# Hybrid encoder layer: when the mLSTM's normalised outputs are transposed, and how many norms are under way

## The chip, the cores and the metric

The kernel runs on one core of a Trainium2 chip. The metric is the device time of one execution in microseconds (us). A time that stands for a kernel is the median of several runs; a profile shows one further execution, which has its own time.

## The reference, cut to what matters

The layer takes two sequences, a prompt of 1024 tokens and a sample of 2048, each with 16 learned meta tokens in front. One projection of the normalised input feeds two branches: attention over a neighbourhood of a grid, and an mLSTM that runs forwards and backwards in 4 heads of 128. Both branches are gated and projected, merged by sigmoid gates, projected once more, normalised and added to the input. This is the part of the mLSTM around the change:

```python
h = (h_f + h_b)[:, :, P:].transpose(0, 2, 1, 3)
h = jax.nn.sigmoid(o_pre.astype(f32)).reshape(B, L, ML_HEADS, ML_HEAD_DIM) * h
mu = jnp.mean(h, axis=-1, keepdims=True)
var = jnp.mean(jnp.square(h - mu), axis=-1, keepdims=True)
h = (h - mu) * lax.rsqrt(var + EPS)
return (h.reshape(B, L, ML_WIDTH) * head_g.astype(f32)).astype(v.dtype)
...
yb = (_mlstm_branch(ml_qk, ml_v, ml_g, ml_o, ml_conv_w, ml_head_g) * jax.nn.silu(ml_z)) @ w_b
```

## The kernel before, in words

**Two streams of work.** The program is written by two Python generators. `dense` writes the large products: the input projection by groups of columns (L422 to L424 token-major, L153 to L155 through `mm3` feature-major), and the final blocks of 512 tokens (`final`, L1255 on: a merge of the two branches, whose products are evacuated from PSUM by VectorE at L1291, L1293 and L1295, and then the output products at L1312 to L1314). `sparse` writes the mLSTM of a sequence (`ml`) and the attention (`na`), in the order of STEPS: mLSTM of the prompt, attention of the prompt, mLSTM of the sample, attention of the sample. Each `yield` of `sparse` ends a *piece* and names a cost (for the mLSTM's outputs A_A = 1.87); `run` then takes as many pieces from `dense` as this cost pays for (six products of 128x512 are 1.41). So a piece of the mLSTM is always followed by products of `dense`, and TensorE runs in the order in which the pieces were written.

**Who orders what.** `manual_schedule` holds for TensorE alone: its queue is the order of the program. The queues of VectorE (DVE), ScalarE (ACT), GpSimd (POOL) and of the DMA issues (SP, SPq in the profile) are ordered by a planner that simulates the program when it is built. On the chip each queue is run in the order that the planner left.

**The mLSTM of one sequence.** For each of four heads, `ml_states` (L915 on, three pieces a block of 256 tokens) makes the states of all chunks, backwards in order, and `ml_outputs` (L1009 on) makes the outputs, a block b of 256 tokens (two chunks) at a time, in six pieces. In iteration b the pieces are: (1) the scores of block b on TensorE (`scores`, PSUM tag sc, one bank) and the start of the next convolution, (2) the products of block b-1's first chunk with state and values (`back`, PSUM tags tr and sm) and the low parts of the scores (L1109), (3) loads, (4) the second chunk (`back`) and the split of the next q (L1049 to L1053), (5) the split of the next k, a decay, and `finish` of block b-1, (6) the other decay and the split of block b's state and values (`state`, L1079 and L1090). The prompt has 4 blocks a head, the sample 8; there is one iteration more than blocks.

`finish` divides the sums into the tile hb (L1144 on ACT, L1145 on DVE). One hb takes two blocks, so every second iteration ends a tile of 512 tokens by one head and puts a generator `ml_norm` (L1192) on the list `norms`. There are 24 such norms: numbers 0 to 7 for the prompt (two a head) and 8 to 23 for the sample (four a head). hb has two buffers. The tiles of the two gates, tog and szg, share two buffers.

**What a norm does, by its own steps.** First step: the sigmoid gate (L1196), four bn_stats (L1200) and four bn_aggr (L1202) on DVE. Second: variance plus epsilon (L1204) and `rsqrt8`, eleven small DVE instructions each of which needs the one before (L139 to L144, three rounds of L142 to L144). Third: four scalings (L1208) and the product with the other gate (L1209), on DVE; then eight empty steps. Last: four transposes on TensorE (L1214, PSUM tag tr, two buffers), the copy back into hb with the head's gain (L1215 on ACT) and the store to HBM (L1216, issued by SP).

**When the steps come.** `ml` drives them (L888 to L903). At each piece the current norm makes one step. A norm that has been put on the list is taken off at the first piece whose step finds no norm under way, and makes its first step one piece after that. It is put on the list in piece 5 of an even iteration b, so its first step comes in piece 6, and its eleventh, with the transposes, in piece 4 of iteration b+2, right behind that piece's `back`. The next norm is put on the list one piece later, so at most one is under way. A norm that is open at the end of a head makes its steps in the pieces of the next head's `ml_states`. After the last head the rest of the steps get a piece each (L902).

Of the kernel before, what the change touches and what calls it, by code (L numbers as in the profile page):

```python
# [120 lines left out]
class K:  # L121
# [748 lines left out]
    def ml(self, s):  # L870
        tc, nc = self.tc, self.nc
        T = SEQLEN[s]
        NB = T // BL
        with tc.tile_pool(name=f"mg{s}", bufs=1, side="right", reuse_waits="tile") as keep:
            with tc.tile_pool(name=f"mt{s}", bufs=1, side="right", reuse_waits="tile") as mp:
                self.tri = keep.tile([P, 2, P], F32, name="tri")
                nc.sync.dma_start(self.tri, self.i["tri"])
                self.trim = keep.tile([P, 2, CB, P], F32, name="trim")
                for j in range(CB):
                    nc.sync.dma_start(self.trim[:, :, j, :], self.i["trimask"])  # L880
                g = []
                yield from self.ml_gates(s, keep, mp, g)
            with tc.tile_pool(name=f"ml{s}", bufs=1, side="right", reuse_waits="tile") as mp:
                self.vas = [mp.tile([P, CB, 130], F32, name=f"va{j}") for j in range(3)]
                for va in self.vas:
                    nc.gpsimd.memset(va[:, :, 128:129], 1.0)
                    nc.gpsimd.memset(va[:, :, 129:130], 0.0)
                norm = iter(())  # L888
                for h in range(4):
                    sts = {}  # L890
                    for cost in self.ml_states(mp, s, h, g, NB, sts):
                        next(norm, None)
                        yield cost
                    norms = deque()
                    for cost in self.ml_outputs(mp, s, h, g, NB, sts, norms):
                        if next(norm, "end") == "end" and norms:
                            norm = norms.popleft()
                        yield cost
                    if norms:
                        for _ in norm:  # L900
                            pass
                        norm = norms.popleft()  # L902
                for _ in norm:  # L903
                    yield A_A
        self.done.add(("ml", s))

# [285 lines left out]
    def ml_norm(self, mp, s, h, q, hb, tz):  # L1192

        nc = self.nc
        to, sz = tz
        nc.vector.scalar_tensor_tensor(hb, to, 1.0, hb, op0=ALU.add, op1=ALU.mult)  # L1196
        bs = mp.tile([P, 4, 6], F32, name="bs", bufs=1)
        mv = mp.tile([P, 4, 2], F32, name="mv", bufs=1)
        for j in range(4):
            nc.vector.bn_stats(bs[:, j], hb[:, j])  # L1200
        for j in range(4):
            nc.vector.bn_aggr(mv[:, j], bs[:, j])  # L1202
        yield
        nc.vector.tensor_scalar(mv[:, :, 1], mv[:, :, 1], 4.0 * EPS, None, op0=ALU.add)  # L1204
        rs = self.rsqrt8(mp, mv[:, :, 1], [P, 4])
        yield
        for j in range(4):
            nc.vector.tensor_scalar(hb[:, j], hb[:, j], mv[:, j, 0:1], rs[:, j:j + 1], op0=ALU.subtract, op1=ALU.mult)  # L1208
        nc.vector.tensor_tensor(hb, hb, sz, op=ALU.mult)  # L1209
        for _ in range(8):  # L1210
            yield
        pt = self.psum("tr", [P, 4, P])
        for j in range(4):
            nc.tensor.transpose(pt[:, j, :], hb[:, j], self.ident)  # L1214
        nc.scalar.activation(hb, pt, AF.Copy, scale=self.hg[:, h:h + 1])  # L1215
        nc.sync.dma_start(self.YB[s][h][:, 512 * q:512 * q + 512], hb.rearrange("p a b -> p (a b)"))  # L1216
# [295 lines left out]
```

## Time and profile before

| | |
|---|---|
| median of 3 runs | 2899.09 us (2895.03 to 2908.92) |
| profiled execution, its time | 2904.42 us |
| profiled execution, its span | 2902.7 us |
| mean granted TensorE clock | 0.989 |
| TensorE products (PE) busy | 2817.5 us, 97% of the span, 17488 instructions |
| TensorE weight loads (PEld) busy | 2510.5 us, 86% |
| DVE busy | 1745.0 us, 60%, 4816 instructions |
| ACT busy | 1297.8 us, 45% |

The span runs from the first to the last instruction; the execution's own time is 1.7 us longer. A line of a group names the line of the kernel, the engine, the operation, the tile written and the tiles read, how often it came, its busy time and mean time, and how long its engine sat idle before it and for whom. In a timeline the first column is the start in us from the span's start and the second the duration. In the table by stretches each engine has its busy time and number of instructions, and PEclk is the share of the full clock that TensorE was granted.

### The profile page before, as it was taken

The numbers are of one execution on the slowest core, as the hardware profiler recorded it, in microseconds if no ns is written. First come the engines' busy times: TensorE is split into PE (matmuls) and PEld (weight loads), VectorE is DVE, ScalarE is ACT, GpSimd is POOL, SyncE is SP. The second block draws the span as 40 slices with busy tenths as digits, with TensorE's granted clock in tenths as the row PEclk, the third lists the DMA queues.
The fourth block names the chain that finished last, engine by engine and source line by source line (L and its number), as shares of the span: only waits on it lengthen the run. The fifth ranks groups of instructions, "written<-read, shape, count | busy, mean of one in ns | idle before, by whom it ended". The sixth has DMA issues, their size and how long they took to land.

```text
span 2902.7 us, 49301 instructions
## 1 busy us (share of the span) xinstructions
PE 2817.5 (97%) x17488; PEld 2510.5 (86%) x17488; DVE 1745.0 (60%) x4816; ACT 1297.8 (45%) x3114; POOL 16.2 (1%) x104
## 2 busy tenths in 40 slices
PE   7999999999999999999998999999999999999998
PEld 6998898899789988888887998898888888879888
DVE  4232575666556754467669877563555557777843
ACT  4112555444443444355555545443444445545421
POOL 0000000000000000000000000000000000000000
PEclk9999999999999999999999999999999999999999
DMA  9655666754775553577678899546669659888875
GB/s 360 213 178 180 209 226 229 270 185 160 246 235 172 185 171 125 174 251 273 233 247 324 284 326 310 160 156 193 188 196 288 202 160 271 256 287 257 292 256 196
DMA packets 387736, 661.88 MB, mean 228 GB/s; under 512 B 50624, under 2 KB 199440, under 8 KB 387488
## 3 DMA queue, kind: packets, MB, share of 16 engines
q1 hardware_dynamic: 386368, 656.03, 68.5%
q0 software_dynamic: 1120, 2.69, 0.4%
q8 instruction: 138, 2.26, 0.3%
q14 instruction: 110, 0.90, 0.1%
HBM read 447.97 MB, written 210.61 MB: 227 GB/s over the span
## 4 chain that ended last, share of the span: by engine, by line
PE 84%; DMA 8%; DVE 5%; issue 1%; ACT 1%; SPq 1%; DVEq 0%; ACTq 0%
PE pj L153 14%; PE pj L154 14%; PE pj L155 14%; PE pj L422 6%; PE pj L424 6%; PE pj L423 6%; PE sm L712 3%; PE pj L1312 3%; PE tr L700 3%; PE pj L1314 3%; PE pj L1313 3%; DMA tg<-gt 1%; PE sc L675 1%; PE sc L676 1%; DMA um<-ud 1%
## 5 line engine op out<-in xcount | busy, mean ns | idle before, releaser
L153 PE MATMUL pj<-xh,whi 128*128 128x512 f32 (+1 forms) x1824 | 717.6, 393 | 0.6 <-ACT xh L324 0.6
L154 PE MATMUL pj<-xl,whi 128*128 128x512 f32 (+1 forms) x1824 | 700.7, 384 | 1.3 <-DVE xl L325 1.3
L155 PE MATMUL pj<-xh,wlo 128*128 128x512 f32 (+1 forms) x1824 | 699.2, 383 | 0.0
L422 PE MATMUL pj<-whi,xh 128*128 128x256 f32 (+3 forms) x1576 | 451.2, 286 | 0.0
L423 PE MATMUL pj<-wlo,xh 128*128 128x256 f32 (+3 forms) x1576 | 445.0, 282 | 0.0
L424 PE MATMUL pj<-whi,xl 128*128 128x256 f32 (+3 forms) x1576 | 444.9, 282 | 0.0
L155 PEld LDWEIGHTS pj<-xh,wlo 128*128 128x128 f32 x1824 | 344.2, 189 | 72.2
L153 PEld LDWEIGHTS pj<-xh,whi 128*128 128x128 f32 x1824 | 344.5, 189 | 57.7 <-ACT xh L324 0.7
L154 PEld LDWEIGHTS pj<-xl,whi 128*128 128x128 f32 x1824 | 345.0, 189 | 56.6 <-DVE xl L325 1.6
L422 PEld LDWEIGHTS pj<-whi,xh 128*128 128x128 f32 (+1 forms) x1576 | 295.2, 187 | 1.4
L423 PEld LDWEIGHTS pj<-wlo,xh 128*128 128x128 f32 (+1 forms) x1576 | 294.6, 187 | 1.1
L424 PEld LDWEIGHTS pj<-whi,xl 128*128 128x128 f32 (+1 forms) x1576 | 294.4, 187 | 0.9
L683 ACT ACTIVATE prb<-sc,mx 128x384 f32<-128x384 f32 (+2 forms) x192 | 120.4, 627 | 228.8 <-DVE mx L679 219.4
L1312 PE MATMUL pj<-whi,mh 128*128 128x256 f32 x768 | 220.0, 286 | 0.0
L1314 PE MATMUL pj<-whi,mlo 128*128 128x256 f32 x768 | 217.2, 283 | 0.9 <-DVE mlo L1295 0.9
L1313 PE MATMUL pj<-wlo,mh 128*128 128x256 f32 x768 | 216.7, 282 | 0.0
L703 DVE TENSOR_TENSOR pts<-tr,pts 96x512 fp32r<-96x512 f32 (+2 forms) x192 | 131.9, 687 | 119.7 <-ACT pts L702 118.1
L431 DVE TENSOR_TENSOR stT<-pj,bb 128x256 f32<-128x256 f32 (+3 forms) x197 | 83.5, 424 | 139.4 <-PE pj L424 136.8
L702 ACT ACTIVATE pts<-tr 96x512 fp32r<-96x512 f32 (+2 forms) x192 | 114.3, 595 | 117.1 <-PE tr L700 116.6
L679 DVE CUSTOM_DVE_ANT_1 sc<-sc,gt 128x384 f32<-128x384 f32 (+2 forms) x192 | 118.7, 618 | 76.0 <-PE sc L676 68.4
L153 PE MATMUL pj<-yh,whi 128*128 128x512 f32 x384 | 157.4, 410 | 4.7 <-DVE tg L1291 4.6
L718 DVE TENSOR_TENSOR yg<-sm,yg 64x128 f32<-64x128 f32 x384 | 108.2, 282 | 77.5 <-ACT yg L716 70.0
(232 smaller groups left out, 5119.5 us busy)
## 6 DMA issues: line engine op xcount, KB each, us to landing
whi<-wh SPq DMA_DIRECT2D x176, 512.0 KB
wlo<-wl SPq DMA_DIRECT2D x176, 512.0 KB
wraw<-wu SPq DMA_DIRECT2D x64, 512.0 KB
wh<-whi SPq DMA_DIRECT2D x64, 512.0 KB
wl<-wlo SPq DMA_DIRECT2D x64, 512.0 KB
gt<-st SPq DMA_DIRECT2D x96, 256.0 KB
tg<-gt SPq DMA_DIRECT2D x96, 256.0 KB
xh<-xh SPq DMA_DIRECT2D x6, 2048.0 KB
```

The lines of the kernel that those rows point to most:

```text
L153: mm(out, ah, bh, start=start, stop=False)
L154: mm(out, ah, bl, start=False, stop=False)
L155: mm(out, al, bh, start=False, stop=stop)
L422: nc.tensor.matmul(o, xh, wh, start=k == 0, stop=False)
L423: nc.tensor.matmul(o, xh, wl, start=False, stop=False)
L424: nc.tensor.matmul(o, xl, wh, start=False, stop=k == KT - 1)
L679: nc.vector.tensor_tensor_reduce(out=so, in0=so, in1=gt[:, g0:g0 + ns, c0:c0 + 32], op0=ALU.add, op1=ALU.min, scale=-1.0, scalar=3.0e38, a ...
L683: nc.scalar.activation(pr_[:, :N].rearrange("p (b a c) -> p b a c", b=4, c=8), sc[:, :N].rearrange("p (a b c) -> p b a c", b=4, c=8), AF.E ...
L703: nc.vector.tensor_tensor(pts[:ks, :, 1, :], pt[:ks], pts[:ks, :, 0, :].bitcast(F32), op=ALU.subtract)
L1312: nc.tensor.matmul(o, mh[:, k, xs], wh, start=k == 0, stop=False)
L1313: nc.tensor.matmul(o, mh[:, k, xs], wl, start=False, stop=False)
L1314: nc.tensor.matmul(o, ml[:, k, xs], wh, start=False, stop=k == KT - 1)
```

## The change

Two things are changed.

In `ml` the one current norm becomes a list of norms under way. At each piece every norm on the list makes one step, and one that ends leaves the list. Nothing waits for an earlier norm to end: a norm put on the list in piece 5 makes its first step in that same piece. The drain at the end of a head (for a norm still open when another is waiting) goes away. After the last head every round makes two steps of each open norm for one piece of cost A_A.

In `ml_norm` the empty steps between the third step and the transposes become twelve instead of eight. A norm now has fifteen steps; the last comes in piece 1 of iteration b+3, right behind that piece's `scores`, or in the next head's `ml_states`. The transposes of a norm come there while the next norm, put on the list in piece 5 of iteration b+2, is already under way.

```diff
-                norm = iter(())
+                norms = deque()
+
+                def step():
+                    for x in tuple(norms):
+                        if next(x, "end") == "end":
+                            norms.remove(x)
+
                 for h in range(4):
                     sts = {}
                     for cost in self.ml_states(mp, s, h, g, NB, sts):
-                        next(norm, None)
+                        step()
                         yield cost
-                    norms = deque()
                     for cost in self.ml_outputs(mp, s, h, g, NB, sts, norms):
-                        if next(norm, "end") == "end" and norms:
-                            norm = norms.popleft()
+                        step()
                         yield cost
-                    if norms:
-                        for _ in norm:
-                            pass
-                        norm = norms.popleft()
-                for _ in norm:
+                while norms:
+                    step()
+                    step()
                     yield A_A
...
         nc.vector.tensor_tensor(hb, hb, sz, op=ALU.mult)
-        for _ in range(8):
+        for _ in range(12):
             yield
         pt = self.psum("tr", [P, 4, P])
```

## The prediction, made before the changed kernel was built or run

> **What bounds the kernel now.** The page first: busy time of the engines.
>
> ```profile
> PE 2817.5 (97%) x17488; PEld 2510.5 (86%) x17488; DVE 1745.0 (60%) x4816; ACT 1297.8 (45%) x3114; POOL 16.2 (1%) x104
> ```
>
> TensorE has a product in flight for 2817.5 us of a span of 2902.7 us. The change neither adds nor takes away a product, so it can only act on the 85 us in which PE has none, and on the clock behind such gaps. The view of PE's waits names them:
>
> ```profile
> PE pj L322 <- DVE xr L311: 18.9, 2, 12.6
> PE tr L1214 <- DVE hb L1209: 12.5, 1, 12.5
> PE tr L700 <- DVE prb L692: 11.3, 3, 6.1
> ```
>
> The first is the start of the program, which the change doesn't touch. The second is the norm's transposes: 24 norms, and one single wait of 12.5 us, for the product L1209 just ahead of them. The third lies in the attention. So 23 of the 24 norms have their transposes at a time when hb is ready, and for them later transposes gain nothing.
>
> The place of the wait, in PE's timeline and in the table by stretches (PE, PEld, DVE, ACT and POOL busy, then PEclk, DMA share, GB/s):
>
> ```profile
> 1554.44 0.28 PE L155 MATMUL sm<-vh,sl 128*128 128x130 f32 x1
> 1567.26 1.08 PE L1214 MATMUL tr<-ident,hb 128*128 128x128 f32 x4 [12.54 <-DVE hb L1209]
> ```
>
> ```profile
> 1500.00:1554.70 54.70, 54.56 (x286) 46.13 (x285) 51.19 (x145) 36.05 (x89) 0.20 (x2) 1.00 0.97 349
> 1554.70:1567.30 12.60, 0.06 (x2) 0.07 (x2) 12.60 (x42) 6.92 (x18) 0.00 (x0) 0.68 0.84 303
> 1567.30:1573.00 5.70, 5.70 (x16) 4.62 (x17) 5.18 (x26) 1.96 (x5) 0.00 (x0) 0.50 0.58 182
> 1573.00:1580.00 7.00, 7.00 (x39) 5.95 (x37) 6.96 (x17) 3.34 (x7) 0.00 (x0) 1.00 0.60 213
> 1580.00:1680.00 100.00, 97.37 (x661) 89.22 (x660) 83.52 (x232) 54.50 (x156) 0.30 (x2) 1.00 0.87 302
> ```
>
> The reader is to see two things. While PE waits, DVE is busy for 12.60 of 12.60 us: the transposes wait for a loaded engine, not for a chain that stands still. And behind the wait PE runs 5.70 us at PEclk 0.50, so that 2.85 us more are lost. The place costs 12.5 + 2.85 = 15.4 us in all, 0.53% of the time. That is the most that the change can win by what it says.
>
> **What the change moves, and the sum.** All is reckoned for norm 13, the one that waits.
>
> *Transposes later: 6.2 us.* They come in piece 1 of an iteration, behind the scores, instead of piece 4 of the one before, behind `back`. What lies between on PE is 24 products of 128x512 and six of the scores. One iteration earlier, at full clock, the same stretch is
>
> ```profile
> 1540.72 0.45 PE L153 MATMUL pj<-yh,whi 128*128 128x512 f32 x1
> ...
> 1546.35 0.22 PE L153 MATMUL sc<-qh,kh 128*128 128x128 f32 x1
> ...
> 1546.96 0.45 PE L153 MATMUL pj<-yh,whi 128*128 128x512 f32 x1
> ```
>
> 1546.96 - 1540.72 = 6.24 us. If L1209 ended when it ends now, the wait would be 12.5 - 6.2 = 6.3 us.
>
> *But DVE gets work in those 6.2 us.* The order of its queue round the wait (each line's first figure is the start):
>
> ```profile
> 1550.13 0.19 DVE L139 TENSOR_SCALAR nwy<-mv 128x4 int32<-128x4 int32 x1
> ...
> 1551.48 0.77 DVE L1102 TENSOR_TENSOR um<-um,sc 128x256 f32<-128x256 f32 x2
> ...
> 1552.53 0.71 DVE L1293 TENSOR_TENSOR tg<-tg 128x512 f32<-128x512 f32 x1
> 1553.14 0.19 DVE L140 TENSOR_SCALAR nwy<-nwy 128x4 int32<-128x4 int32 x1
> ...
> 1554.88 0.18 DVE L142 SCALAR_TENSOR_TENSOR nwt<-nwy 128x4 f32<-128x4 f32 x1
> 1554.95 0.71 DVE L1295 TENSOR_TENSOR mlo<-tg,mh 128x512 fp32r<-128x512 f32 x1
> ...
> 1556.07 0.71 DVE L1291 SCALAR_TENSOR_TENSOR tg<-tg,pj 128x512 f32<-128x512 f32 x1
> 1556.67 0.19 DVE L143 TENSOR_TENSOR nwt<-nwt,mv 128x4 f32<-128x4 f32 x1
> ...
> 1566.41 0.70 DVE L1209 TENSOR_TENSOR hb<-hb,szg 128x512 f32<-128x512 f32 x1
> ...
> 1570.94 0.69 DVE L1291 SCALAR_TENSOR_TENSOR tg<-tg,pj 128x512 f32<-128x512 f32 x1
> ...
> 1575.46 0.69 DVE L1291 SCALAR_TENSOR_TENSOR tg<-tg,pj 128x512 f32<-128x512 f32 x1
> ```
>
> The eleven small steps of the reciprocal root take 0.2 us each but stand 1.7 to 3.0 us apart, because evacuations, splits and scores stand between them. Today the evacuations of the 24 products behind the wait come after L1209 (1570.94, 1575.46), because PE stood still. In the new order PE makes these products first, and the planner may let their evacuations in ahead of L1209: two L1291, one L1293, one L1295 (0.71 each) and the two L1102 of the scores (0.77), 3.6 us. The ends are 0 (all stay behind) and 3.6 (all go ahead). The nearest row is L1291 at 1556.07, which went between two steps of the root 2.3 us after its products ended; so I take 3.6 and keep 0.
>
> *The norm's steps one piece earlier.* The first step is written in piece 5 instead of 6. What it needs is the second half of hb:
>
> ```profile
> 1538.40 0.35 DVE L1145 SCALAR_TENSOR_TENSOR hb<-num,den,hb 128x128 f32<-128x128 f32 x1
> ...
> 1540.87 0.69 DVE L1196 SCALAR_TENSOR_TENSOR hb<-tog,hb 128x512 f32<-128x512 f32 x1
> ```
>
> hb is there at 1538.75 and L1196 starts at 1540.87. So the chain can start between 0 and 2.1 us earlier; other ready work will stand ahead of it here too, and I take half, 1.0.
>
> *The sum.* New wait: 12.5 - 6.2 + 3.6 - 1.0 = 8.9 us, a gain of 3.6. The ends are 12.5 - 6.2 - 2.1 = 4.2 (gain 8.3) and 12.5 - 6.2 + 3.6 = 9.9 (gain 2.6). The half clock stays: a much shorter stop has one behind it as well.
>
> ```profile
> 1233.00:1235.00 2.00, 0.09 (x1) 0.00 (x0) 2.00 (x7) 2.00 (x8) 0.10 (x1) 1.00 0.47 114
> 1235.00:1242.00 7.00, 5.82 (x26) 5.52 (x27) 5.48 (x18) 4.45 (x16) 0.00 (x0) 0.51 0.45 113
> ```
>
> Two microseconds with almost no product, and then 7 us at 0.51, worth 3.5 us. [...]
>
> *What costs nothing, and what hides it.* The number of instructions is the same. PSUM's tr pair: the transposes now stand between two `back`s six pieces apart, with more room than now. The gates' buffers are read by the first and third step as before. The last norm of each sequence: two steps a piece make its transposes come after six pieces instead of nine, so the lead of hb shrinks. It is now
>
> ```profile
> 754.90 0.69 DVE L1209 TENSOR_TENSOR hb<-hb,szg 128x512 f32<-128x512 f32 x1
> ```
>
> ```profile
> 770.89 0.60 PE L1214 MATMUL tr<-ident,hb 128*128 128x128 f32 x4
> ```
>
> 15.3 us over nine pieces, so a third less leaves some 10: no wait. The store L1216 and hb's buffer: the store goes out 6.2 us later, and the ACT write of the norm after next waits for its landing. The tightest pair, and a transfer of the same 256 KB on the chain of waits:
>
> ```profile
> 1776.78 0.35 SPq L1216 DMA_DIRECT2D yb<-hb  x1
> ```
>
> ```profile
> 1784.94 0.69 ACT L1144 ACTIVATE hb<-num,den 128x128 f32<-128x128 f32 x2
> ```
>
> ```profile
> 1537.93 6.49 DMA tg<-gt
> ```
>
> 1776.8 + 6.2 + 6.5 = 1789.5, so ACT could stand 4.6 us at that one norm, with everything in its queue behind it (the next block's decay, the sums of `back`). ACT is 45% busy and PE asks for these only pieces later; I take 0 and keep 4.6 for the range. On SP, the store is moved past about two loads of the next block, each 0.3 to 0.4 us to issue: nothing.
>
> On the profiled execution this gives 2904.4 - 3.6 = 2900.8 us. Its own time lies 5.3 us above the median of 2899.1 (runs from 2895.0 to 2908.9), and the prediction is for the median: **2895.5 us**, 2890 to 2898 by the ends.
>
> **The rivals.** *The wait goes altogether.* The product would have to end at 1554.7 + 6.2 = 1560.9 instead of 1567.1. For it: the planner makes DVE's order anew, and between 1554.7 and 1567.3 DVE also did work of the next head, which nothing waits for. Against it: DVE was full. Gain 15.4 us, 2883.7 us; it decides if the planner's order brings the chain 6.2 us forward.
>
> *The wait is handed on.* DVE is busy 51.19 + 12.60 + 5.18 + 6.96 + 83.52 = 159.5 us between 1500 and 1680; without the 15.4 us that is 97% of what is left. If DVE is the limit there, PE stops for the same work a little later, at `tg` or `mlo`: 2899 us, and the change doesn't do what it says.
>
> *Slower: the norm pushes the state split back.* The first step now stands ahead of `state(b)` in the program instead of behind it, and the second beside it. PE needs the split (vl, L1079) two pieces later in `back`, and its lead is thin in places:
>
> ```profile
> 1519.80 0.43 DVE L1079 TENSOR_TENSOR vl<-va,vh 128x260 fp32r<-128x260 f32 x1
> ```
>
> ```profile
> 1521.74 0.28 PE L153 MATMUL tr<-cch,qh 128*128 128x260 f32 x1
> ```
>
> ```profile
> 1567.02 0.88 DVE L1200 BATCH_NORM_STATS2 bs<-hb 128x6 f32<-128x128 f32 x4
> ...
> 1568.18 0.39 DVE L1202 BATCH_NORM_AGGREGATE mv<-bs 128x2 f32<-128x6 f32 x4
> ```
>
> The lead is 1521.74 - 1520.23 = 1.5 us. The first step is 0.69 + 0.88 + 0.39 = 2.0 us and the root eleven times 0.18, 2.0: 4.0 us ahead of vl leave PE 2.5 us short, and the half clock of the rows at 1235 adds 3.5: 6.0 us a place. Sixteen of the 24 norms have such a split behind them (one a head in the prompt, three in the sample). It decides from three places on: with the gain of 3.6, three give 2913.5 and four 2919.5; I take 2916. Against it: this lead is among the thinnest, and hb itself, which the first step needs, comes late. For it: the planner lays out three queues anew for every product that moves, and one wrong order has cost 15.4 us here. [...]
>
> **How the numbers follow.** Forecast 0.36, wait gone 0.25, handed on 0.12, slower 0.27. A measurement of this kernel can tell about 0.5%, 14.5 us, from no change. Faster by more than that is the case of the wait gone, 0.25 (2883.7 is just past the bound of 2884.6); within it lie the forecast and the handed-on wait, 0.48; slower by more, 0.27. The range goes from 2880 (the wait gone and a third of L700's 11.3 us with it) to 2917 (three places, and the 4.6 us of ACT for the most part): it leaves out half of the slower case and little below.
>
> **What would show it.** Right: PE's wait at L1214 for L1209 is one, 4 to 10 us long, at norm 13, with PEclk 0.50 behind it; L1291 stands between the steps of the root after 1557. Gone: no row L1214 among PE's waits. Handed on: a new row of `pj` for `tg` or `mlo` of about 10 us between 1555 and 1600. Slower: rows of `back` (tr or sm, L153 or L154) for vl or ccl, which today has none. Wrong altogether: the difference lies outside the mLSTM's stages, in L700 or L322, where only the planner's order and the balance of the two streams changed (four pieces fewer).

## The result, and the profile after

| | before | changed |
|---|---|---|
| median of 12 runs | 2903.11 us | 2897.55 us |
| lowest and highest | 2895.03 to 2908.92 us | 2891.70 to 2900.43 us |
| ratio (95% interval) | | 0.9978 (0.997 to 0.9987) |
| profiled execution: time, span | 2904.42, 2902.7 us | 2893.49, 2891.7 us |

The change makes the kernel 0.22% faster: 5.6 us between the medians, where 3.6 were forecast. That is less than the 0.5% that the prediction thought could be told from no change, and with twelve runs each it is still clear of noise: the interval leaves out 1. The profiled executions lie 10.9 us apart, twice as far as the medians; a second profile of each program, further down, shows how much of that is chance.

The page's busy times, and the head of the list of PE's waits, of the changed kernel (its lines behind `ml` stand two further down, so L1216 is the transposes, L1293 the first evacuation of the merge):

```profile
PE 2813.2 (97%) x17488; PEld 2507.9 (87%) x17488; DVE 1743.7 (60%) x4816; ACT 1293.7 (45%) x3114; POOL 16.2 (1%) x104
```

```profile
PE pj L322 <- DVE xr L311: 18.4, 2, 12.1
PE tr L1216 <- DVE mv L1204: 9.7, 1, 9.7
PE sc L675 <- ACT kd L655: 6.9, 1, 6.9
PE pj L322 <- DVE xl L325: 6.2, 6, 1.8
PE tr L700 <- DVE prb L692: 4.6, 4, 2.2
PE sm L763 <- issue: 4.4, 1, 4.4
PE pj L153 <- DVE tg L1293: 4.3, 2, 2.6
```

The row of before for kd, the keys at the start of the prompt's attention:

```profile
PE sc L675 <- ACT kd L655: 1.8, 1, 1.8
```

Read against the rows of before, three things have changed. The wait at the transposes is still one, at norm 13, and has gone from 12.5 to 9.7 us (it is put down to L1204, a small instruction of the next norm that ended at the same moment; the product in front of the transposes, L1211, ended at 1576.27, 0.15 us before them). The wait for kd is now 6.9 us; it was 1.8. And the waits of the attention's transposes, L700, have gone from 11.3 to 4.6 us.

Norm 13 in the changed kernel, as PE's timeline and as a table by stretches:

```profile
1565.92 0.22 PE L153 MATMUL sc<-qh,kh 128*128 128x128 f32 x1
...
1566.42 0.27 PE L155 MATMUL sc<-qh,kl 128*128 128x128 f32 x1
1576.42 0.87 PE L1216 MATMUL tr<-ident,hb 128*128 128x128 f32 x3 [9.72 <-DVE mv L1204]
```

```profile
1555.00:1566.60 11.60, 11.60 (x60) 9.73 (x59) 11.60 (x31) 7.61 (x20) 0.00 (x0) 1.00 1.03 391
1566.60:1576.40 9.80, 0.10 (x1) 0.01 (x1) 9.80 (x36) 4.36 (x12) 0.00 (x0) 0.61 0.92 304
1576.40:1583.00 6.60, 6.58 (x24) 5.80 (x25) 6.22 (x24) 4.89 (x12) 0.00 (x0) 0.55 0.77 250
```

The transposes do come behind the scores, as written, and DVE is busy for the whole of the wait, 9.80 of 9.80 us, as it was before. Half clock follows again (0.55 over 6.6 us).

By stage, the two kernels in the same three stretches (the prompt's attention starting, the sample's mLSTM beside the first final blocks, the sample's attention beside the last ones). Before:

```profile
780.00:830.00 50.00, 46.21 (x226) 37.48 (x225) 23.32 (x52) 23.50 (x46) 0.00 (x0) 0.97 0.93 306
1480.00:1700.00 220.00, 203.50 (x1202) 178.49 (x1201) 184.91 (x518) 124.28 (x325) 0.50 (x4) 0.97 0.86 302
2268.00:2840.00 572.00, 554.58 (x3276) 486.58 (x3275) 395.65 (x934) 257.16 (x603) 1.02 (x2) 0.99 0.79 251
```

After:

```profile
780.00:830.00 50.00, 40.91 (x192) 33.13 (x191) 22.18 (x47) 20.87 (x41) 0.00 (x0) 0.90 0.84 268
1480.00:1700.00 220.00, 210.26 (x1242) 185.76 (x1241) 184.85 (x525) 125.83 (x333) 0.51 (x4) 0.97 0.87 305
2268.00:2840.00 572.00, 562.41 (x3338) 493.77 (x3336) 397.59 (x931) 255.32 (x599) 1.02 (x2) 0.99 0.79 254
```

PE without a product: 3.8 against 9.1 us in the first stretch (5.3 lost), 16.5 against 9.7 in the second (6.8 won), 17.4 against 9.6 in the third (7.8 won). So more than half of what these two profiles show as won lies in the attention, where the change moves no norm. That asks for a second theory.

### The profile page after: what moved, and what is told of

Read it like the earlier page. It is cut to its first block, busy times and chain, and to the rows that moved or that the text cites. A ratio compares the mean times of both kernels' runs of the same rounds, so it can differ in the third digit from the quotient of the medians.

```text
span 2891.7 us, 49311 instructions
## 1 busy us (share of the span) xinstructions
PE 2813.2 (97%) x17488; PEld 2507.9 (87%) x17488; DVE 1743.7 (60%) x4816; ACT 1293.7 (45%) x3114; POOL 16.2 (1%) x104
## 4 chain that ended last, share of the span: by engine, by line
PE 82%; DVE 7%; DMA 7%; ACT 1%; issue 1%; SPq 1%; DVEq 0%; ACTq 0%
PE pj L153 14%; PE pj L154 14%; PE pj L155 14%; PE pj L422 6%; PE pj L423 6%; PE pj L424 6%; PE sm L712 3%; PE pj L1314 3%; PE pj L1316 3%; PE pj L1315 3%; PE tr L700 3%; DMA um<-ud 2%; PE sc L675 1%; PE sc L676 1%; PE sm L155 1%
```

## The experiments

**The theories.** *Wait*: the gain is the shorter wait at norm 13, because its transposes come later. *Balance*: the gain comes from the other thing the change does, the two steps a piece after the last head. It takes two pieces from each end, so `sparse` pays for 3.7 units less of `dense` twice, and from there on each piece of `sparse` meets an earlier product of `dense`. *Chance*: the profiles differ as executions of one program do.

A unit of the attention is one piece of it that begins with a score product L675; the prompt has 64 and the sample 128. Counted in the order of PE's queue, with a narrower product counted by its share of 512 columns, the products of the dense stream ahead of the first unit of the prompt are 2835 before and 2817 in the changed kernel; ahead of the first unit of the sample (the 65th in all), 6993 and 6963. This lag, 18 and then 30 products, is what the experiments vary. It is the lag at the first unit; at later units it goes mostly between 12 and 18 where it began at 18, mostly between 30 and 36 where it began at 30, and mostly between 42 and 48 where it began at 48.

`after_again`, `tail9` and `comb` start from the changed kernel. All others start from the program of before written with the new driver, and their diffs are against that: the first step of a norm waits one piece more, eight empty steps, nine pieces at the ends. Its order on every queue is that of before. The lines that make it so, against the changed kernel:

```diff
+        late = False
+        if not late:
+            yield
...
-        for _ in range(12):
+        for _ in range(12 if late else 8):
...
                 while norms:
                     step()
-                    step()
-                    yield A_A
+                    if norms:
+                        yield A_A
```

**Chance: two more profiles, `before_again` and `after_again`.** The program of before in that form, and the changed kernel, with no further edit.

> The program of before, written with the new driver, one more profile. It tells how far two profiles of one program lie apart. If waits are set by the order of the queues, the wait at norm 13 is again 12 to 13 us and the attention's waits at L700 again about 11 us. If they are set by how the transfers fell in that one execution, they differ by several us.

> The changed kernel, one more profile. If its waits are set by the order of the queues, the wait at norm 13 is again 9 to 10 us, that for kd 6 to 7 us and those at L700 4 to 5 us; if by the one execution, they differ by several us.

Measured: 2899.10 and 2901.42 us, one execution each, so that in this pair the changed kernel is the slower one by 2.3 us. The wait at norm 13 is 12.9 and 9.2 us, that for kd 1.3 and 8.2, L700 9.2 and 4.4. So the three waits belong to the programs, within some 2 us; of the 10.9 us between the first two profiles about half was chance. Two profiles of before show where such chance sits, and where it does not. In the first 40 us they were granted different clocks:

```profile
0.00:40.00 40.00, 19.12 (x115) 18.09 (x116) 26.66 (x65) 20.98 (x37) 1.38 (x19) 0.87 0.96 347
```

```profile
0.00:40.00 40.00, 20.33 (x113) 19.19 (x114) 26.58 (x65) 20.89 (x36) 1.38 (x19) 1.00 0.97 354
```

One execution was granted 0.87 of the clock there and the other all of it, and yet PE started 115 products in the first and 113 in the second: half of the stretch PE waits, and the lower clock cost nothing that lasts. The first unit of the sample's attention starts at almost the same time in both:

```profile
2018.68 0.34 PE L675 MATMUL sc<-kd,stk 128*128 128x384 f32 x1
```

```profile
2018.51 0.34 PE L675 MATMUL sc<-kd,stk 128*128 128x384 f32 x1
```

The spans are 2902.7 and 2897.3 us, so nearly all of the 5.4 us between the two came behind this point. The stretch from 2268 to 2840 us, where the change seems to win most, is also the one in which executions of one program differ most.

**The two parts apart: `only13`, `tail7`, `tail9`.** `only13` gives the new times to the one norm that waits:

```diff
         to, sz = tz
-        late = False
+        late = (s, h, q) == (1, 1, 1)
         if not late:
             yield
```

> Only norm 13, the one that waited, gets the new times of its steps; the other 23 norms and the ends of the two mLSTM stages stay as before. If the shorter wait at the transposes is the gain (the prediction's theory), the wait falls from 12.5 to some 9 or 10 us and the median is 2 to 4 us below before, a ratio near 0.999. If the gain of the whole change comes from the planner's new order at the other places, this kernel is within 1 us of before, whatever its wait does.

Measured: ratio 1.0001 (0.9989 to 1.0013), medians 2902.03 and 2901.81 us. The wait:

```profile
PE tr L1219 <- DVE mv L1207: 12.4, 1, 12.4
```

```profile
1552.70:1559.00 6.30, 6.30 (x33) 5.24 (x32) 6.30 (x17) 4.91 (x12) 0.00 (x0) 1.00 0.97 343
1559.00:1571.50 12.50, 0.20 (x2) 0.06 (x1) 12.50 (x42) 5.28 (x14) 0.00 (x0) 0.67 0.98 349
```

PE has the 6.3 us of products in front of the transposes and then waits as long as before. The wait was handed on whole. Why is read from DVE's timeline of this kernel (L1296, L1298 and L1300 are the evacuations of the merge, L1104 and L1111 the scores, L1214 the norm's product):

```profile
1558.76 0.69 DVE L1296 SCALAR_TENSOR_TENSOR tg<-tg,pj 128x512 f32<-128x512 f32 x1
...
1560.42 0.17 DVE L142 SCALAR_TENSOR_TENSOR nwt<-nwy 128x4 f32<-128x4 f32 x1
1560.50 0.70 DVE L1300 TENSOR_TENSOR mlo<-tg,mh 128x512 fp32r<-128x512 f32 x1
...
1561.17 1.23 DVE L240 TENSOR_TENSOR wlo<-wraw,whi 128x1024 fp32r<-128x1024 f32 x1
1562.31 0.69 DVE L1296 SCALAR_TENSOR_TENSOR tg<-tg,pj 128x512 f32<-128x512 f32 x1
...
1563.30 0.76 DVE L1104 TENSOR_TENSOR um<-um,sc 128x256 f32<-128x256 f32 x2
1563.96 0.17 DVE L143 TENSOR_TENSOR nwt<-nwt,mv 128x4 f32<-128x4 f32 x1
...
1565.11 0.18 DVE L144 SCALAR_TENSOR_TENSOR nwy<-nwt,nwy 128x4 f32<-128x4 f32 x1
1565.19 0.44 DVE L1111 TENSOR_TENSOR sl<-um,sh 128x256 fp32r<-128x256 f32 x1
...
1570.01 0.90 DVE L1205 BATCH_NORM_STATS2 bs<-hb 128x6 f32<-128x128 f32 x4
1570.79 0.71 DVE L1214 TENSOR_TENSOR hb<-hb,szg 128x512 f32<-128x512 f32 x1
```

The two evacuations that stood behind the product in before (1570.94 and 1575.46 there) now stand in front of it, between the steps of the root. From the norm's first step to its product, both counted, DVE has 94 instructions instead of the 79 of `before_again`: two more L1296, one more L1298, L1300 and L240 each, two L1104 and two L1111 more, one more each of L865 and L940, which belong to the next head's convolutions, and four bn_stats of the next norm (L1205). The first step and the product in `before_again`:

```profile
1539.97 0.68 DVE L1201 SCALAR_TENSOR_TENSOR hb<-tog,hb 128x512 f32<-128x512 f32 x1
...
1565.51 0.69 DVE L1214 TENSOR_TENSOR hb<-hb,szg 128x512 f32<-128x512 f32 x1
```

and the first step in `only13`:

```profile
1539.10 0.69 DVE L1201 SCALAR_TENSOR_TENSOR hb<-tog,hb 128x512 f32<-128x512 f32 x1
```

From the first step's start to the product's end it is 26.2 us in `before_again` and 32.4 us in `only13`: 6.2 us more, as much as PE comes later. The first step itself, though written one piece earlier, follows the same three instructions of DVE's queue in both kernels (L1296, L1300, L1111).

`tail7` keeps the old times of all norms and shortens only the ends:

```diff
-                while norms:
+                for n in range(7):
                     step()
-                    if norms:
-                        yield A_A
+                    if n < 3:
+                        step()
+                    yield A_A
```

> The norms' steps come as before (eight empty steps, first step one piece late), but after the last head of each sequence the rest of the steps are made in seven pieces instead of nine, as in the changed kernel. If the gain lies in the wait at norm 13, this kernel keeps that wait of about 12.5 us and its time is within 2 us of before. If the gain comes from the two streams meeting in another way after the shorter end, it has most of the changed kernel's gain, 4 to 6 us, with a longer wait for kd at the start of the attention (6.9 us instead of 1.8) and shorter waits at the attention's transposes late in the run.

Measured: ratio 0.9980 (0.997 to 0.999), medians 2896.55 and 2901.81 us: by these runs the whole gain of the change, with no norm's transposes moved but the two at the ends. Its three stretches:

```profile
780.00:830.00 50.00, 40.76 (x194) 33.31 (x193) 22.92 (x50) 21.45 (x43) 0.00 (x0) 0.90 0.84 269
1480.00:1700.00 220.00, 208.21 (x1225) 183.56 (x1225) 186.33 (x526) 125.80 (x333) 0.50 (x4) 0.97 0.87 303
2268.00:2840.00 572.00, 562.58 (x3359) 494.34 (x3358) 397.29 (x932) 256.11 (x603) 1.02 (x2) 1.00 0.78 254
```

They are those of the changed kernel, but for 2 us in the second. The wait for kd is 7.3 us, L700 5.5; at norm 13 PE waits 8.7 us and at norm 12 another 1.7.

`tail9` is the rest: the changed kernel's norms, all 24, with the ends put back to nine pieces:

```diff
-                while norms:
-                    step()
-                    step()
-                    yield A_A
+                for n in range(10):
+                    step()
+                    if n < 3:
+                        step()
+                    if n < 9:
+                        yield A_A
```

> The changed kernel with the cost at the ends of both mLSTM stages put back to nine pieces, so that all 24 norms have the new times of their steps and the streams meet as before. If the balance of the streams is the whole gain, it is within 2 us of before, with 11 to 13 us of wait at norm 13, as when that norm alone was moved. If moving all norms takes load off DVE at the right time, the wait is 9 to 10 us and it is 2 to 4 us below before.

Measured: ratio 1.0008 (0.9997 to 1.0018), medians 2905.35 and 2903.80 us; the wait at norm 13 is 12.1 us. So the two things that the change is about, twelve steps and two norms under way, give nothing that can be measured by themselves. *Wait* has fallen as the cause of the gain.

**Balance or earlier stores: `cost7`.** The ends keep nine pieces, each with 7/9 of the cost:

```diff
                 while norms:
                     step()
                     if norms:
-                        yield A_A
+                        yield A_A * 7 / 9
```

> Both ends keep nine pieces with one step of the norm each, but a piece there has 7/9 of the cost, so the dense stream is taken on as far as with seven. If the balance of the two streams is what matters, it runs as the kernel with seven pieces does: 4 to 7 us below before, wait for kd 6 to 8 us, L700 4 to 6 us. If it matters that the last norm's transposes and store come earlier, it is within 2 us of before.

Measured: ratio 0.9984 (0.9974 to 0.9995), medians 2896.87 and 2902.93 us. The wait for kd is 8.2 us, L700 4.8. It has the lag of the short ends (2817 and 6963 products) and not their number of pieces, and runs as they do.

**Which end, and how much: `s0`, `s1`, `s1c5`, `s1c3`.** `s0` and `s1` shorten one end alone to seven pieces, the prompt's or the sample's; `s1c5` and `s1c3` leave the prompt's end alone and multiply the cost at the sample's:

```diff
-                while norms:
+                short = s == 0
+                for n in range(7 if short else 10):
                     step()
-                    if norms:
+                    if short and n < 3:
+                        step()
+                    if n < 9:
                         yield A_A
```

(`s1` has `short = s == 1`), and `s1c5` (`s1c3` with 3 for 5):

```diff
                     if norms:
-                        yield A_A
+                        yield A_A * (5 / 9 if s else 1)
```

> The program of before, but the end of the prompt's mLSTM alone is shortened to seven pieces. By the theory of the balance it has the longer wait for kd at the start of the prompt's attention, 7 to 8 us, with half clock behind it, so it loses some 8 us there, and half of the shift late: it is slower than the kernel with both ends short, and between 4 us slower and 2 us faster than before. If the prompt's end is what gains late, it is as fast as with both ends short, 5 to 6 us below before.

> The program of before, but the end of the sample's mLSTM alone is shortened to seven pieces; the prompt's end keeps nine. If the gain late in the attention comes from the balance of the two streams there, and each end moves it by 3.7 units of cost, half of the shift is made here: a gain of 3 to 10 us without the 6 us that the short end of the prompt's mLSTM loses at the start of its attention; the wait for kd stays at 1.8 us and L700 falls below 9 us. If the gain needs the whole shift of 7.5 units or comes from the prompt's end, the time is within 2 us of before.

> The program of before with the cost of the nine pieces at the end of the sample's mLSTM cut to 5/9 and the prompt's end left alone. From the sample's attention on, TensorE then has as many products of the dense stream behind it at each unit as in the changed kernel (6963 products of 128x512 at the 65th unit, against 6993 before), while the prompt's attention starts as before. If the late balance is the cause, the stretch from 2268 us to the end is 10 to 13 us shorter than before, the wait for kd stays at 2 us, and the median is 9 to 14 us below before (ratio 0.995 to 0.997), faster than the changed kernel. If the gain needs the shift at the prompt's end as well, it is within 2 us of before.

> As s1c5, with 3/9: the dense stream is 48 products behind before at the 65th unit (6945). If a longer lag always helps, it is faster than with 5/9. If what counts is which work of the final blocks falls on which unit of the attention, the time goes up and down with the lag (18 products made it slower, 30 faster), and it may lie anywhere from 8 us slower to 15 us faster than before.

The table has for each kernel the lag of the dense stream behind before at the start of the prompt's and of the sample's attention, in products of 128x512, the measured ratio, the wait at norm 13 (with that at norm 12 where there is one), and the time that PE lost in the three stretches of the tables by stretches: its idle time, plus half of its busy time under half clock by the trace's record of the clock (an estimate: in before, products of 128x512 started 0.43 us apart at 0.50 behind the wait at norm 13, and 0.23 us apart from 1573 us on, at 1.00). A stretch of fixed times does not hold the same work in every kernel. So the last column gives the time from the start of the first unit of the sample's attention to the end of the span, less 0.232 us for each product that the lag leaves to be made there (the median distance from one such product to the next in the profile of before). Each kernel was run beside the program of before, whose median so differs from group to group. `n2` and `comb` are described below.

```
kernel         lag   ratio (95%)              wait 13    780:830  1480:1700  2268:2840  from unit 65
before         0, 0  -                        12.5         5.5      19.4       24.3     884.0
before_again   0, 0  -                        12.9         4.1      20.3       20.3     878.8
only13         0, 0  1.0001 (0.9989, 1.0013)  12.4         4.2      18.6       17.9     878.1
tail9          0, 0  1.0008 (0.9997, 1.0018)  12.1         7.6      18.0       22.9     883.4
n2             0, 0  0.9987 (0.9977, 0.9998)  11.2         7.0      17.9       27.1     886.4
s0            18,18  1.0021 (1.0009, 1.0033)  8.7 + 2.6   11.8      16.3       22.3     880.6
s1             0,18  1.0024 (1.0012, 1.0036)  12.9         5.2      21.9       22.1     883.3
tail7         18,30  0.9980 (0.9970, 0.9990)  8.7 + 1.7   12.4      15.4        9.4     867.4
cost7         18,30  0.9984 (0.9974, 0.9995)  8.7 + 2.1   15.0      17.6      15.8     873.9
after         18,30  0.9978 (0.9970, 0.9987)  9.7         13.0      12.7       12.8     869.9
after_again   18,30  -                        9.2         13.5      12.4       15.9     873.7
s1c5           0,30  0.9974 (0.9962, 0.9985)  12.9         5.7      19.0       13.3     872.4
s1c3           0,48  0.9999 (0.9989, 1.0009)  12.9         4.4      19.3       20.6     879.5
comb           0,30  0.9977 (0.9967, 0.9987)  13.0         5.2      19.2       15.5     876.4
```

The time lost goes with the lag. A lag of 18 at the prompt's attention costs about 8 us there on average, and the kernels that have it lose less in the sample's mLSTM (12 to 18 us, the others 18 to 22); the wait at norm 13 goes below 10 us in just these kernels, whether the transposes moved or not. With the old norms part of it turns up at norm 12 instead: the two come to 10.4 to 11.3 us, where the changed norms have 9.2 to 9.7. So on top of this lag, but not without it, the moved transposes seem to win something in the mLSTM; the medians of the changed kernel and `tail7` do not show it (0.9978 and 0.9980).

A lag of 30 at the sample's attention leaves 9 to 16 us lost instead of 18 to 27, and from unit 65 to the end these kernels take 867 to 876 us, all others 878 to 886. The two groups nearly touch (876.4 and 878.1), and the two profiles of before differ by 5, but the ratios say the same: the five kernels with a lag of 30 have 0.9974 to 0.9984, and the others 0.9987 (`n2`, whose norms do less) and more. A lag of 18 there or of 48 does not help: the effect goes up and down. `s0` came out 4.3 us slower than before (medians 2907.27 and 2902.93), a little more than the 4 us that were expected at most; what it loses at the prompt's attention and wins in the mLSTM is of that size. `s1` came out 6.3 us slower (2909.23 and 2902.93), against what was expected, and its one profile does not show where that time goes. `s1c3` is 1.4 us below before (2902.36 and 2903.80). Where the time sits in that stretch changes with the lag. In `s1` it is the scores, which wait for the exponentials of the unit before:

```profile
PE sc L675 <- ACT prb L683: 8.3, 5, 3.4
PE tr L700 <- DVE prb L692: 5.4, 2, 2.9
PE pj L153 <- DVE tg L1299: 2.7, 2, 2.3
```

In `s1c3` it is the transposes again and the merge:

```profile
PE tr L700 <- DVE prb L692: 7.0, 2, 5.1
PE pj L153 <- DVE tg L1296: 3.8, 4, 1.8
PE pj L1319 <- DVE mlo L1300: 3.2, 2, 1.8
```

`s1c5` has the lag of 30 without the one of 18 in the prompt. Its ratio, 0.9974, stands for the late gain without the loss at the prompt's attention, and without the gain at the mLSTM; it is not told apart from the changed kernel. That its median would be 9 to 14 us below before was too much: it is 7.7 (2896.10 and 2903.80).

**Both together: `comb`.** The changed kernel's norms, with `tail9`'s rounds at the ends and 5/9 of the cost at the sample's. Against `tail9`:

```diff
                     if n < 9:
-                        yield A_A
+                        yield A_A * (5 / 9 if s else 1)
```

> The changed kernel's norms, the prompt's end at nine pieces, the sample's end at 5/9 of their cost. If the gains add up, it has the late gain of 10 to 13 us, no loss at the prompt's attention, and the 0 to 3 us of the norms: 10 to 15 us below before, 4 to 9 us below the changed kernel.

Measured: ratio 0.9977 (0.9967 to 0.9987), medians 2896.55 and 2903.80 us, 7.3 us below before and not 10 to 15. The norms' part adds nothing to `s1c5` that shows: without the lag in the prompt the wait at norm 13 is 13.0 us.

**What sets the wait: `n2`.** One Newton round of three left out of the root of every norm. Each round also multiplies the value by about -2 (L144 takes t - 3, with t near 1), and the code behind counts on all three; so the norms of this kernel have the other sign and half the size, and its time alone is of use:

```diff
-        for n in range(3):
+        for n in range(steps):
...
-        rs = self.rsqrt8(mp, mv[:, :, 1], [P, 4])
+        rs = self.rsqrt8(mp, mv[:, :, 1], [P, 4], 2)
```

> The program of before without the third round of the norm's reciprocal root, three small dependent DVE instructions of 0.2 us for each norm; the norms' values differ by that round. If the wait at norm 13 is made by a chain of small steps each of which stands behind 1.7 to 3.0 us of other work, it falls from 12.5 by 5 to 9 us, to 4 to 8 us. If it is made by the amount of work that DVE has ahead, it falls by 0.6 us, to about 12.

Measured: ratio 0.9987 (0.9977 to 0.9998), medians 2900.81 and 2902.93 us.

```profile
PE tr L1219 <- DVE hb L1214: 11.2, 1, 11.2
```

Three dependent steps fewer, which stood 1.7 to 3.0 us apart, take 1.3 to 1.7 us off the wait: less than the 5 to 9 of the chain, more than the 0.6 of the amount of work. The chain does not set the wait alone; the work that stands in DVE's queue does for the most part. DVE's order was made anew here too, which this run does not tell apart.

## Why the prediction was right in number and wrong in its reason

That 3.6 us were forecast and 5.6 measured is luck. Everything named as a mark of being right was seen (one wait of 4 to 10 us at norm 13, half clock behind it with 0.55 over 6.6 us, L1291 between the steps of the root), and so was the mark of being wrong altogether: a difference in L700, outside the mLSTM. The pair of profiles could not decide between them; the experiments did.

- **What bounds the kernel** was read rightly: PE's products, one wait of 12.5 us at the norms, with half clock behind it (0.50 for 5.70 us), and DVE full during it (12.60 of 12.60 us). The forecast of a wait of 8.9 us at norm 13 looks met by 9.7. It is not the wait made shorter by later transposes alone: with those alone it is 12.4 (`only13`) and 12.1 (`tail9`).
- **The step "But DVE gets work in those 6.2 us"** failed by its size. The term was 3.6 us, for two L1291, one L1293, one L1295 and the two L1102, and was called the upper end. All of these did go ahead, but so did an L240, two L1109, the next norm's bn_stats and parts of the next head's convolutions: the term is 6.2 us (32.4 instead of 26.2 from the first step to the product). The next term, "The norm's steps one piece earlier", was 1.0 us and is nothing, as the first step kept its place in DVE's queue. With these sizes the sum is 12.5 - 6.2 + 6.2 = 12.5 us, and 12.4 was measured.
- **The step "What costs nothing, and what hides it"** failed for the ends of the two mLSTM stages. The two pieces fewer were weighed by the lead of hb alone, which did hold (11.2 and 7.6 us are left for norms 7 and 23, no wait). That fewer pieces put the dense stream 18 and 30 products back was named only as a mark of being wrong altogether. It is the gain: 0.9980 by itself.
- **"The wait is handed on"**, given 0.12, comes nearest to what happens to the norms' part, though not by its sign: the wait did not pass to `tg` or `mlo`, it stayed at the transposes. The other rivals did not come about: the wait did not go, and no row of `back` waits for vl above 0.3 us.
- **The range** "2890 to 2898 by the ends" is not what its ends give: gains of 8.3 and 2.6 us from 2899.1 are 2890.8 and 2896.5.
- **hb's buffers** cost nothing, as said: among ACT's waits before hb in the changed kernel there is none for the store.
- **The clock** did as the prediction took it from the rows: behind the 9.7 us PE ran at 0.55 for 6.6 us, which is some 6 us of half clock; in before it was 5.70 us at 0.50 behind the 12.5 us. The sum took the half clock as the same in both kernels.

What stays open: why a lag of 30 products fits the sample's attention and 18 and 48 do not. The rows show which waits come and go, not which final block's work must miss which unit. Every lag also made the planner lay out the queues of DVE, ACT and SP anew, and no run holds these still, so the products met and the order of the other queues are not told apart. And `tail9` and `only13` bound the norms' part within some 0.1 to 0.2%, not at exactly nothing.

## What to carry to other kernels

When a consumer waits for an engine that is full, moving the consumer later can let more work into that engine's queue ahead of what it waits for, and the wait stays; here the planner did that for the whole 6.2 us. Before counting the microseconds moved, list everything that the producer's queue will get in that time. A change that also alters how many pieces one stream takes shifts every meeting of two interleaved streams behind it, and this can outweigh the change itself: vary that shift alone (here, the cost of a piece) before crediting the edit. The effect of such a shift went up and down here (18 products slower, 30 faster, 48 the same), so the best value has to be found by trying; that it carries over to another version of the kernel is not shown.

## What the runs showed of the hardware that was not expected

In the first 40 us a lower granted clock cost no time that shows: two executions of one program were granted 0.87 and 1.00 there, and PE, idle for half of that stretch in both, started 115 and 113 products in it (rows above). What set the two executions 5.4 us apart came in the sample's attention and the end. With runs of one program between 2895 and 2912 us, two single profiles cannot show a gain of 0.2%, and the second pair of profiles even came out the other way round; a stretch can be compared only where two profiles of the same program agree on it.
